# A decoder trunk on one core: in a step of seven products, the fifth goes to SBUF and is added from there

## The chip, the cores and the metric

The kernel runs on one core of one Trainium2 chip. The metric is device time in microseconds (us) of one execution, lower is better. Engines are named as the profile names them: PE is TensorE's matmul side (PEld its weight loads), DVE is VectorE, ACT is ScalarE, POOL is GpSimd, SP is SyncE, which issues most DMAs.

## The reference

The program is a decoder trunk of two layers for one sequence of 512 tokens and a width of 1024, all in float32. Each layer does

```
h = RMSNorm(x)
p = h @ W_in                     # columns shared by four head groups
y = concat[retention(p), conformer_conv(p), gated_deltanet(p), hgrn2(p)]
x = x + y @ W_out
x = x + SwiGLU(RMSNorm(x))       # silu(x @ W_gate) * (x @ W_up), then @ W_down; hidden width 2816
```

and a last RMSNorm follows. The mixers are causal and work in chunks along the sequence. The change lies in the last line, the feed-forward part.

## The kernel before, in words

Activations lie transposed: 128 rows of the width on the partitions, the 512 tokens along the free axis. So x is eight tiles of 128x512, and the hidden width is 22 tiles, j = 0 to 21. A product in float32 is made of two halves of each operand, a high part (rounded to the type fp32r) and the rest: `mm3` issues three matmuls for it, high by high (L461), high weight by low activation (L462), low weight by high activation (L463). Weights come by DMA into `wraw`; ScalarE makes the high half (L257, L383) and GpSimd or VectorE the low half (L258, L384). PSUM has two pools of four banks of 128x512 each: `pm` and `pd`.

**The step of seven products.** In the feed-forward part most tiles are made in pairs by a scheme in the manner of Strassen: the gate and up products of one j, or two output tiles of the down projection, take seven products of half the width (256 tokens) instead of eight. Their names are e, t1, t2, g, h, t3, t4. The weights of these products are the quarters a, b, d of a pair and the differences s1 to s4, which `s_item` computes ahead on VectorE and GpSimd (L366, L370, L374, L378). The activations are sums of token halves, made by `operand` for the gate and up products and by `blocks_even` and `blocks_odd` (with `split`, L1567 to L1569) for the down products. A product is 12 matmuls of 128x256: four blocks by three.

`step` (from L1636) makes one such pair. It takes two banks of `pm`: `ab` and `cd`, each with a lower half LO (256 columns) and an upper half UP. In order:

- e into the lower half of cd; ScalarE copies it to the lower half of gs, in SBUF (L1648)
- t1 into the upper half of ab; ScalarE copies it on (L1650; the change is here)
- `finish()` runs the last part of the step before: its t4 into its cd, and its `second` function
- t2 is accumulated on e in the lower half of cd; ScalarE copies the sum to the upper half of gs (L1653)
- g into the lower, h into the upper half of ab; VectorE adds gs to ab (L1656); `first(ab)` uses the result: Silu into sg on ScalarE for a hidden tile, an addition to x for a down tile
- t3 is accumulated in the lower half of cd; the upper half of cd becomes e+t2+t3 plus t1 (L1659 and L1660; the change is here)
- later, in `end`: t4 is accumulated in the lower half of cd, and `second(cd)` uses the whole bank. For a hidden tile it multiplies with sg (L1677, or in place at L1673) and splits the result for the down products (`hidden_split`, L1583 to L1585 and L1568, L1569); for a down tile it adds to x.

**Where the steps stand.** In each layer j = 0 to 3 are made plainly, j = 4 to 21 by `step` (18 steps), and down tiles by `step` in two parts of four (8 steps), with plain down products (`down_plain`, width 512, into banks of `pd`) for the first and the last tiles. So there are 26 steps in a layer and 52 in the program. Ahead of the feed-forward part of a layer come its mixers, many small operations between dense products: the gated deltanet, called gdn in the code, has chains such as L1082, L1090, L1099, L1112, hgrn2 and the others theirs.

**What sets the order.** Each engine runs its instructions in one fixed order. That order is not the order of the code: the program is built with a scheduler that simulates a timeline (`schedule_with_timeline_sim=True`, L1823) and places instructions by it, within dependencies. An edit therefore also moves instructions that it does not name. The wait of an instruction is for whole tiles or parts of them; a matmul into a half of a bank has to wait for an operation of another engine that writes or reads the bank and stands ahead of it.

Of the kernel before, what the change touches and what calls it, by code (L numbers as in the profile page):

```python
# [7 lines left out]
F32 = mybir.dt.float32  # L8
# [8 lines left out]
P = 128  # L17
# [121 lines left out]
def kernel(  # L139
# [15 lines left out]
    V, S, GP, PE = nc.vector, nc.scalar, nc.gpsimd, nc.tensor  # L155
    MUL, ADD, SUB = ALU.mult, ALU.add, ALU.subtract
# [257 lines left out]
    def w_next(keep=0):  # L414

        i = pos[2]
        pos[2] += 1
        for q in held.values():
            q[:] = [n for n in q if n >= i - keep]
        p = piece_of(items[i])  # L420
        w_split(i + 1)
        assert i in halves
        w_load(p + 3)
        w_split(i + 2)
        while pos[1] < min(i + 1 + AHEAD, len(items)) and len(items[pos[1]]) == 2 and extra:
            n = pos[1]
            w_split(n + 1)
            if pos[1] == n:
                break
            w_load(piece_of(items[n]) + 3)  # L430
        return halves.pop(i)
# [27 lines left out]
    def mm3(ps, hi, lo, kk, ah, al, first, last, shared=False):  # L459
        w = slice(kk * P, (kk + 1) * P)  # L460
        PE.matmul(ps, hi[:, w], ah, start=first, stop=False, skip_group_check=shared)  # L461
        PE.matmul(ps, hi[:, w], al, start=False, stop=False, skip_group_check=shared)  # L462
        PE.matmul(ps, lo[:, w], ah, start=False, stop=last, skip_group_check=shared)  # L463
# [1028 lines left out]
    for l in range(DEPTH):  # L1492
# [47 lines left out]
        with tc.tile_pool(name=f"ffp{l}", bufs=1, reuse_waits="tile") as ffp, \  # L1540
# [3 lines left out]
            HC = T // 2  # L1544
            LO, UP = slice(0, HC), slice(HC, T)
# [84 lines left out]
            def finish():  # L1630

                for f in last:
                    f()
                last.clear()

            def step(of, first, second):  # L1636

                def product(ps, nm, start=False):
                    hi, lo = w_next()
                    for k in range(KD // 2):  # L1640
                        mm3(ps, hi, lo, k, *of(k, nm), start and k == 0, k == KD // 2 - 1, True)

                ab = pm.tile([P, T], F32, name="pm")
                cd = pm.tile([P, T], F32, name="pm")
                gs = fft.tile([P, T], F32, name="gs")
                u3 = fft.tile([P, HC], F32, name="u3")
                product(cd[:, LO], "e", True)
                S.copy(gs[:, LO], cd[:, LO])  # L1648
                product(ab[:, UP], "t1", True)
                S.copy(cd[:, UP], ab[:, UP])  # L1650
                finish()
                product(cd[:, LO], "t2")
                S.copy(gs[:, UP], cd[:, LO])  # L1653
                product(ab[:, LO], "g")
                product(ab[:, UP], "h")
                V.tensor_tensor(ab, ab, gs, op=ADD)  # L1656
                first(ab)
                product(cd[:, LO], "t3")
                S.copy(u3, cd[:, LO])  # L1659
                V.tensor_tensor(cd[:, UP], cd[:, UP], u3, op=ADD)  # L1660

                def end():
                    product(cd[:, LO], "t4")
                    second(cd)
                last.append(end)

            def hidden(j):
                sg = fft.tile([P, T], F32, name="sg")

                def up(cd):  # L1670
                    if j in rest and j != rest[0]:
                        raw[j] = cd
                        V.tensor_tensor(cd, cd, sg, op=MUL)  # L1673
                        hidden_split(j)
                    else:
                        raw[j] = sqp.tile([P, T], F32, name="sq")
                        V.tensor_tensor(raw[j], cd, sg, op=MUL)  # L1677
                        if (j - HEAD) % PART:
                            hidden_split(j)
                step(of_x, lambda ab: S.activation(sg, ab, AF.Silu), up)  # L1680

            def down(part, q):
                def add(m):
                    return lambda ps: V.tensor_tensor(x[m], x[m], ps, op=ADD)
                step(of_hidden, add(2 * q), add(2 * q + 1))
                if q == KD // 2 - 1:

                    last.append(lambda: hidden_split(HEAD + PART * (part + 1)))
# [138 lines left out]
```

## Time and profile before

| | us |
|---|---|
| three runs | 1333.13, 1335.5, 1335.95 |
| median | 1335.5 |
| the profiled execution | 1333.43 |
| its span in the trace | 1331.6 |
| ScalarE instructions in the span | 1454, busy 705.5 |

The mean granted clock of TensorE in the profiled execution was 0.978 of full speed. How rows are read: a row of a timeline has the start in us, the duration in us, engine, line, operation, the tile written and the tiles read, the shape, and in brackets the idle time of the engine ahead of it and what ended that. Tile names are without numbers there, so `pm<-pm` can be two different banks. A row of a source line has the count and the shortest, median and longest duration in ns. A row of waits has the line that waited, the line that it waited for, us in total, times, and the longest in us. Matmuls are pipelined, so their durations overlap: the next one can start before the end of the last.

In the trace the steps of layer 0 run from 383 us to some 655 us, and those of layer 1 from 1030 us to some 1304 us; the mixers of layer 1 lie between some 700 us and 945 us.

### The profile page before, as it was taken

The numbers are of one execution on the slowest core, as the hardware profiler recorded it, in microseconds if no ns is written. First come the engines' busy times: TensorE is split into PE (matmuls) and PEld (weight loads), VectorE is DVE, ScalarE is ACT, GpSimd is POOL, SyncE is SP. The second block draws the span as 40 slices with busy tenths as digits, with TensorE's granted clock in tenths as the row PEclk, the third lists the DMA queues.
The fourth block names the chain that finished last, engine by engine and source line by source line (L and its number), as shares of the span: only waits on it lengthen the run. The fifth ranks groups of instructions, "written<-read, shape, count | busy, mean of one in ns | idle before, by whom it ended". The sixth has DMA issues, their size and how long they took to land.

```text
span 1331.6 us, 23717 instructions
## 1 busy us (share of the span) xinstructions
PE 1287.8 (97%) x8984; PEld 1177.3 (88%) x8984; DVE 897.5 (67%) x1569; ACT 705.5 (53%) x1454; POOL 788.4 (59%) x669
## 2 busy tenths in 40 slices
PE   8999998899999999999999999999999999999996
PEld 6888887888889999999888889889788999999995
DVE  5753778646787867876465448686559777678645
ACT  5553543535456656655545435445444665566554
POOL 6376773753255765676545767747523666566762
PEclk9999998899999999999999999889999999999998
DMA  7223210134043333342542232002423243333322
GB/s 270 79 79 105 75 25 9 41 111 134 25 135 96 111 112 96 97 126 80 164 138 80 81 88 67 25 1 71 154 69 103 80 123 102 110 97 110 122 78 72
DMA packets 60386, 124.52 MB, mean 94 GB/s; under 512 B 17520, under 2 KB 26992, under 8 KB 60272
## 3 DMA queue, kind: packets, MB, share of 16 engines
q1 hardware_dynamic: 58832, 121.83, 30.0%
q8 instruction: 71, 1.16, 0.4%
q10 hardware_dynamic: 1440, 1.18, 0.3%
q14 instruction: 43, 0.35, 0.1%
HBM read 116.17 MB, written 6.82 MB: 92 GB/s over the span
## 4 chain that ended last, share of the span: by engine, by line
PE 82%; DVE 8%; POOL 5%; ACT 3%; issue 2%; DMA 0%; SPq 0%; POOLq 0%; ACTq 0%; DVEq 0%
PE pm L461 12%; PE pm L462 12%; PE pm L463 12%; PE pd L461 10%; PE pd L462 10%; PE pd L463 10%; PE pd L486 2%; PE pm L1189 2%; PE pd L488 2%; PE pd L487 2%; POOL wlo L258 2%; DVE x L1292 1%; PE pm L928 1%; ACT whi L383 1%; PE pm L1062 1%
## 5 line engine op out<-in xcount | busy, mean ns | idle before, releaser
L258 POOL TENSOR_TENSOR wlo<-wraw,whi 128x512 fp32r<-128x512 f32 (+2 forms) x192 | 248.9, 1305 | 227.3 <-ACT whi L257 186.7
L384 POOL TENSOR_TENSOR wlo<-wraw,whi 128x512 fp32r<-128x512 f32 x208 | 272.5, 1329 | 104.4 <-ACT whi L383 99.9
L461 PE MATMUL pm<-bh,whi 128*128 128x256 f32 x1008 | 282.5, 282 | 3.9 <-ACT pm L1650 2.0
L462 PE MATMUL pm<-bl,whi 128*128 128x256 f32 x1008 | 281.2, 280 | 0.0
L463 PE MATMUL pm<-bh,wlo 128*128 128x256 f32 x1008 | 276.5, 280 | 0.0
L257 ACT CAST whi<-wraw 128x512 fp32r<-128x512 f32 (+2 forms) x212 | 125.3, 598 | 188.1 <-PE pd L462 105.1
L461 PEld LDWEIGHTS pm<-bh,whi 128*128 128x128 f32 x1008 | 189.6, 188 | 6.8 <-DVE pm L1660 3.1
L462 PEld LDWEIGHTS pm<-bl,whi 128*128 128x128 f32 x1008 | 190.0, 188 | 0.5
L463 PEld LDWEIGHTS pm<-bh,wlo 128*128 128x128 f32 x1008 | 187.8, 189 | 0.1
L383 ACT CAST whi<-wraw 128x512 fp32r<-128x512 f32 x208 | 126.7, 624 | 50.1 <-PE pm L462 42.7
L461 PE MATMUL pd<-xh,whi 128*128 128x512 f32 x384 | 151.6, 396 | 0.6 <-DVE x L729 0.6
L463 PE MATMUL pd<-xh,wlo 128*128 128x512 f32 x384 | 151.9, 396 | 0.0
L462 PE MATMUL pd<-xl,whi 128*128 128x512 f32 x384 | 151.6, 396 | 0.0
L384 DVE TENSOR_TENSOR wlo<-pd,whi 128x512 fp32r<-128x512 f32 x156 | 107.3, 688 | 52.4 <-ACT whi L383 49.9
L383 ACT CAST whi<-pd 128x512 fp32r<-128x512 f32 x156 | 92.0, 590 | 64.9 <-PE pm L462 22.6
L378 POOL TENSOR_TENSOR wraw<-wraw 128x512 f32<-128x512 f32 x52 | 68.8, 1324 | 78.2 <-DVE pd L366 65.9
L486 PE MATMUL pd<-whi,xh 128*128 128x256 f32 (+1 forms) x320 | 94.2, 295 | 8.0 <-DVE x L1292 3.4
L487 PE MATMUL pd<-wlo,xh 128*128 128x256 f32 (+1 forms) x320 | 93.7, 293 | 0.0
L488 PE MATMUL pd<-whi,xl 128*128 128x256 f32 (+1 forms) x320 | 93.5, 293 | 0.0
L461 PEld LDWEIGHTS pd<-xh,whi 128*128 128x128 f32 x384 | 72.3, 188 | 16.7 <-DVE x L729 0.8
L462 PEld LDWEIGHTS pd<-xl,whi 128*128 128x128 f32 x384 | 72.2, 188 | 16.0
L463 PEld LDWEIGHTS pd<-xh,wlo 128*128 128x128 f32 x384 | 72.2, 188 | 15.9
(359 smaller groups left out, 3181.0 us busy)
## 6 DMA issues: line engine op xcount, KB each, us to landing
wraw<-in_wf_dram SPq DMA_DIRECT2D x88, 512.0 KB, 3.6
wraw<-in_wc_dram SPq DMA_DIRECT2D x34, 512.0 KB, 3.6
wraw<-in_wd_dram SPq DMA_DIRECT2D x32, 512.0 KB, 4.0
wraw<-in_wt_dram SPq DMA_DIRECT2D x16, 512.0 KB, 3.6
wraw<-in_wo_dram SPq DMA_DIRECT2D x32, 256.0 KB, 2.6
x<-in_xt_dram SPq DMA_DIRECT2D x16, 256.0 KB, 3.7
wraw<-in_wd_dram SPq DMA_DIRECT2D x16, 256.0 KB, 2.7
wraw<-in_wd_dram SPq DMA_DIRECT2D x20, 128.0 KB, 2.0
```

What stands on the lines that cost most here:

```text
L257: S.copy(hi[:, :n], r)
L258: eng.tensor_tensor(lo[:, :n], r, hi[:, :n].bitcast(F32), op=SUB)
L378: GP.tensor_tensor(src, c, a, op=SUB)
L383: S.copy(hi, src)
L384: eng.tensor_tensor(lo, src, hi.bitcast(F32), op=SUB)
L461: PE.matmul(ps, hi[:, w], ah, start=first, stop=False, skip_group_check=shared)
L462: PE.matmul(ps, hi[:, w], al, start=False, stop=False, skip_group_check=shared)
L463: PE.matmul(ps, lo[:, w], ah, start=False, stop=last, skip_group_check=shared)
L486: PE.matmul(o, xh[k][:, tk], hi[:, w], start=(k == 0 and first), stop=False)
L487: PE.matmul(o, xh[k][:, tk], lo[:, w], start=False, stop=False)
L488: PE.matmul(o, xl[k][:, tk], hi[:, w], start=False, stop=(k == KD - 1 and last))
L1189: PE.matmul(ps[:, (bb * 2 + ct) * P:(bb * 2 + ct + 1) * P], k[:, ct * T + b * P:ct * T + (b + 1) * P], qx[:, (ct * NB + b) * P:(ct * NB + ...
```

## The change: t1 to SBUF, one addition instead of copy and addition

Before, ScalarE copied t1 from its bank ab into the upper half of the bank cd, and after t3 it copied the lower half of cd to an SBUF tile u3, which VectorE added to the upper half. Now ScalarE copies t1 to an SBUF tile p5 (same size, same pool, two buffers), and after t3 VectorE writes the sum of the lower half of cd and p5 to the upper half. The second copy is gone. What is computed stays the same.

```diff
                 gs = fft.tile([P, T], F32, name="gs")
-                u3 = fft.tile([P, HC], F32, name="u3")
+                p5 = fft.tile([P, HC], F32, name="u3")
                 product(cd[:, LO], "e", True)
                 S.copy(gs[:, LO], cd[:, LO])
                 product(ab[:, UP], "t1", True)
-                S.copy(cd[:, UP], ab[:, UP])
+                S.copy(p5, ab[:, UP])
                 finish()
...
                 product(cd[:, LO], "t3")
-                S.copy(u3, cd[:, LO])
-                V.tensor_tensor(cd[:, UP], cd[:, UP], u3, op=ADD)
+                V.tensor_tensor(cd[:, UP], cd[:, LO], p5, op=ADD)
```

The changed file is one line shorter there, so L1660 of before is L1659 of after. ScalarE has 52 copies fewer; the other engines have the same instructions in another order. TensorE's order is the same up to the first steps of layer 0; from there on the steps, and the mixers of layer 1, are placed anew. Four places show it.

First TensorE, from the end of t1 of j=7 on. Before, pm_4154 is ab and pm_4155 is cd of j=7, pm_4007 is cd of j=6, and a row with waits names the engine that the matmul waits for:

```order
L463 MATMUL pm_4154<-bh3_3174,wlo_4081 128x256
L461 MATMUL pm_4155<-bh0_3168,whi_4115 128x256 [waits Activation_49]
...
L463 MATMUL pm_4155<-bh3_3174,wlo_4116 128x256
L461 MATMUL pm_4154<-bh0_3168,whi_4135 128x256
L462 MATMUL pm_4154<-bl0_3169,whi_4135 128x256
L461 MATMUL pm_4007<-bh0_3168,whi_4099 128x256 [waits DVE_49]
```

After, the same tiles are pm_4151 (ab), pm_4152 (cd of j=7) and pm_4005 (cd of j=6):

```order
L463 MATMUL pm_4151<-bh3_3174,wlo_4079 128x256
L461 MATMUL pm_4005<-bh0_3168,whi_4097 128x256 [waits DVE_49,Activation_49]
...
L463 MATMUL pm_4005<-bh3_3174,wlo_4098 128x256
L461 MATMUL pm_4152<-bh0_3168,whi_4113 128x256 [waits Activation_49]
...
L463 MATMUL pm_4152<-bh3_3174,wlo_4114 128x256
L461 MATMUL pm_4151<-bh0_3168,whi_4133 128x256 [waits Activation_49]
```

Before, t2 of j=7 follows t1 directly, and t4 of j=6 comes after it, between the matmuls of g; after, t4 of j=6 stands between t1 and t2.

Second VectorE, in the step of j=8. Before, pm_4297 is ab and pm_4298 is cd; the rows of L384, L370 and L374 work on weights of later products:

```order
L384 TENSOR_TENSOR wlo_4372<-pd_4373,whi_4371 128x512 [waits Activation_49]
L370 TENSOR_TENSOR pd_4408<-wraw_4199,pd_4373 128x512 [waits DMAHW7_49]
L1656 TENSOR_TENSOR pm_4297<-pm_4297,gs_4299 128x512 [waits PE_49]
L384 TENSOR_TENSOR wlo_4407<-pd_4408,whi_4406 128x512 [waits Activation_49]
L374 TENSOR_TENSOR pd_4451<-wraw_4199,pd_4408 128x512 [waits DVE_49]
L1660 TENSOR_TENSOR pm_4298<-pm_4298,u3_4300 128x256 [waits Activation_49]
```

After, they are pm_4293 and pm_4294:

```order
L384 TENSOR_TENSOR wlo_4368<-pd_4369,whi_4367 128x512 [waits Activation_49]
L370 TENSOR_TENSOR pd_4404<-wraw_4196,pd_4369 128x512 [waits DMAHW7_49]
L1656 TENSOR_TENSOR pm_4293<-pm_4293,gs_4295 128x512 [waits PE_49]
L1659 TENSOR_TENSOR pm_4294<-pm_4294,u3_4296 128x256 [waits PE_49]
L384 TENSOR_TENSOR wlo_4403<-pd_4404,whi_4402 128x512 [waits Activation_49]
L374 TENSOR_TENSOR pd_4446<-wraw_4196,pd_4404 128x512 [waits DVE_49]
```

The addition into the upper half now follows L1656 directly and waits for TensorE; L384 and L374 come behind it.

Third TensorE at the end of the steps of layer 0. Before, pm_7258 is cd of j=21; the first row is the end of its t3, the row with whi_7356 the start of its t4, and the last row the first plain down product that needs the result (ph6):

```order
L463 MATMUL pm_7258<-bh3_3174,wlo_7281 128x256
L462 MATMUL pd_7420<-ph1_3177,whi_7404 128x512
...
L462 MATMUL pd_7472<-ph5_3181,whi_7449 128x512
L461 MATMUL pm_7258<-bh0_3168,whi_7356 128x256 [waits DVE_49]
...
L463 MATMUL pm_7258<-bh3_3174,wlo_7357 128x256
L463 MATMUL pd_7472<-ph4_3180,wlo_7450 128x512
L461 MATMUL pd_7374<-ph6_3182,whi_7383 128x512 [waits Activation_49]
```

After, the bank is pm_7233:

```order
L463 MATMUL pm_7233<-bh3_3174,wlo_7256 128x256
L462 MATMUL pd_7348<-ph3_3179,whi_7327 128x512
...
L463 MATMUL pd_7394<-ph4_3180,wlo_7379 128x512
L461 MATMUL pm_7233<-bh0_3168,whi_7331 128x256 [waits DVE_49]
...
L463 MATMUL pm_7233<-bh3_3174,wlo_7332 128x256
L463 MATMUL pd_7420<-ph0_3176,wlo_7398 128x512 [waits Pool_49]
...
L463 MATMUL pd_7446<-ph4_3180,wlo_7424 128x512
L461 MATMUL pd_7348<-ph6_3182,whi_7357 128x512 [waits Activation_49]
```

Between t3 and t4 there were 25 plain down matmuls and are now 16; between t4 and the first matmul that reads ph6 there was one and are now 16.

Fourth, TensorE in the mixers of layer 1, at a chain of the gated deltanet. Before, with dense products into banks of pd between the links:

```order
L1189 MATMUL pm_8880<-ar4_7_8648,ar4_3_8117 128x128 [waits PE_49]
...
L463 MATMUL pd_9362<-xh6_90,wlo_9261 128x512
...
L461 MATMUL pd_9492<-xh5_89,whi_9358 128x512
L1090 MATMUL pm_8892<-ar2_7_8410,ar2_10_8415 128x64 [waits DVE_49,PE_49]
...
L462 MATMUL pd_9492<-xl5_97,whi_9358 128x512
...
L463 MATMUL pd_9492<-xh7_91,wlo_9359 128x512
L1099 MATMUL pm_8907<-ar2_7_8410,ar4_3_8140 128x128 [waits Activation_49]
```

After, with further matmuls of the same lines left out:

```order
L1082 MATMUL pm_8847<-gS0_175,ar4_1_7682 128x128 [waits DVE_49]
...
L1189 MATMUL pm_8854<-ar4_7_8622,ar4_3_8091 128x128 [waits PE_49]
...
L1090 MATMUL pm_8866<-ar2_7_8384,ar2_10_8389 128x64 [waits DVE_49,Activation_49]
...
L1099 MATMUL pm_8881<-ar2_7_8384,ar4_3_8114 128x128 [waits Activation_49]
...
L1112 MATMUL pm_8888<-ar2_7_8384,ar2_1_7595 128x64 [waits DVE_49]
```

Before, 20 dense matmuls (width 512) stood between L1189 and L1090, and 8 between L1090 and L1099; they now come ahead of the chain.

## The prediction

> **What bounds the kernel now.** I read the page first (busy times, chain), then the windows of the feed-forward stages, then what TensorE waited for, and last the timelines around those waits.
>
> ```profile
> span 1331.6 us, 23717 instructions
> PE 1287.8 (97%) x8984; PEld 1177.3 (88%) x8984; DVE 897.5 (67%) x1569; ACT 705.5 (53%) x1454; POOL 788.4 (59%) x669
> PE 82%; DVE 8%; POOL 5%; ACT 3%; issue 2%; DMA 0%; SPq 0%; POOLq 0%; ACTq 0%; DVEq 0%
> ```
>
> TensorE is busy for 97% of the span and makes up 82% of the chain that ended last. The next two rows are stretches of feed-forward steps, one in each layer (columns: busy time of PE, PEld, DVE, ACT, POOL with counts; granted clock; DMA share; GB/s).
>
> ```profile
> 404.00:640.00 236.00, 234.20 (x1970) 232.62 (x1969) 170.40 (x281) 143.77 (x309) 152.85 (x118) 1.00 0.34 101
> 1060.00:1300.00 240.00, 238.08 (x1986) 235.51 (x1985) 169.42 (x279) 145.35 (x311) 157.03 (x121) 1.00 0.35 104
> ```
>
> In the steps TensorE idles 1.8 and 1.9 us in about 240, at full clock; a matmul follows the last after 234.20 / 1970 = 0.119 us. The change removes no matmul, so all that it can gain there is idle time of TensorE. That time is named in the waits of PE (us in total, times, longest):
>
> ```profile
> PE pd L461 <- ACT ph L1568: 2.3, 2, 1.2
> PE pm L461 <- ACT pm L1650: 2.0, 4, 0.5
> PE pm L461 <- DVE pm L1660: 1.9, 6, 0.4
> ```
>
> Twelve waits, 6.2 us together. All three kinds hang on lines that the edit touches: the copy of the fifth product, the addition into the upper half, and the chain behind the last t4.
>
> **Part by part: the copies.** These rows give the lines' cost (ns min/median/max), the last one for how long VectorE sat idle ahead of the addition, and how often, until the copy L1659 was done.
>
> ```profile
> L1650 ACT COPY pm<-pm x52: 357/375/396, 386.2 to 1287.3; 128x256 f32<-128x256 f32 x52
> L1659 ACT COPY u<-pm x52: 365/372/380, 395.5 to 1296.7; 128x256 f32<-128x256 f32 x52
> L1660 DVE TENSOR_TENSOR pm<-pm,u x52: 418/432/433, 396.0 to 1297.1; 128x256 f32<-128x256 f32 x52
>   ACT u L1659: 22.4, 27
> ```
>
> The t1 copy now writes SBUF as L1659 did, so I price it at 0.372 instead of 0.375 us: nothing. L1659's 52 copies go: 52 x 0.372 = 19.3 us of ScalarE. ScalarE is busy 53%, so by itself this gives nothing; it counts only where a matmul waited behind it. The addition keeps its shape, one PSUM and one SBUF operand: 0.432 us as before. Its wait is new: for TensorE's last t3 matmul, not for ScalarE. Behind it in VectorE's queue stand weight splits (L384, L374) for products still to come; at those 27 places the addition starts earlier by the copy's 0.4 us, so they come no later. At the others VectorE has a backlog and the addition waits for nothing: nothing again.
>
> **Place 1: t2 behind the t1 copy** (j=7; four such waits in the kernel).
>
> ```profile
> 415.89 0.28 PE L463 MATMUL pm<-bh,wlo 128*128 128x256 f32 x1
> 416.26 0.36 ACT L1650 COPY pm<-pm 128x256 f32<-128x256 f32 x1 [0.20 <-PE pm L463]
> 416.67 0.39 PE L461 MATMUL pm<-bh,whi 128*128 128x256 f32 x1 [0.50 <-ACT pm L1650]
> 416.90 0.28 PE L462 MATMUL pm<-bl,whi 128*128 128x256 f32 x1
> ```
>
> The copy wrote the upper half of the bank into whose lower half t2 goes, so t2 waited. The wait costs more than its 0.50: from 415.89 to 416.90 are two intervals, 1.01 - 2 x 0.119 = 0.77, so 0.27 us of restart comes with it. I add 0.27 to each of the twelve. In the changed order the copy no longer touches that bank, and t2 of j=7 depends on it no more; what still waits for it is the next writer of the bank that it reads (g or h). The nearest of these stands 14 matmuls behind t1, 14 x 0.119 = 1.67 us, against 416.67 - 415.89 = 0.78 that the copy needed here from the last t1 matmul to the release. Gain 2.0 + 4 x 0.27 = 3.1 us.
>
> **Place 2: t4 close behind t3** (j=4 of each layer).
>
> ```profile
> 395.55 0.38 ACT L1659 COPY u<-pm 128x256 f32<-128x256 f32 x1
> 395.93 0.28 PE L462 MATMUL pm<-bl,whi 128*128 128x256 f32 x1
> 395.96 0.43 DVE L1660 TENSOR_TENSOR pm<-pm,u 128x256 f32<-128x256 f32 x1 [0.62 <-ACT u L1659]
> 396.45 0.39 PE L461 MATMUL pm<-bh,whi 128*128 128x256 f32 x1 [0.23 <-DVE pm L1660]
> ```
>
> The chain copy, addition, t4 loses its first link, 395.96 - 395.55 = 0.41 us, more than the 0.23 waited. In the changed order 24 instead of 12 matmuls also stand between t3 and this t4, 1.4 us more. Both waits go.
>
> **Place 3: the addition late in VectorE's queue** (j=8; four such waits, behind odd j whose splits fill VectorE).
>
> ```profile
> 428.28 0.69 DVE L1677 TENSOR_TENSOR sq<-pm,sg 128x512 f32<-128x512 f32 x1
> 435.26 0.38 ACT L1659 COPY u<-pm 128x256 f32<-128x256 f32 x1
> 435.40 0.69 DVE L384 TENSOR_TENSOR wlo<-pd,whi 128x512 fp32r<-128x512 f32 x1
> 436.01 0.69 DVE L374 TENSOR_TENSOR pd<-wraw,pd 128x512 f32<-128x512 f32 x1
> 436.46 0.28 PE L463 MATMUL pm<-bh,wlo 128*128 128x256 f32 x1
> 436.60 0.42 DVE L1660 TENSOR_TENSOR pm<-pm,u 128x256 f32<-128x256 f32 x1
> 437.08 0.38 PE L461 MATMUL pm<-bh,whi 128*128 128x256 f32 x1 [0.34 <-DVE pm L1660]
> ```
>
> Here the copy was done by 435.64; the addition started only at 436.60, after L384 and L374. So dropping the copy would gain nothing: what gains is that the new order puts the addition ahead of those two, 436.60 - 435.40 = 1.20 us earlier, against 0.34 waited. With place 2 the six waits on L1660 give 1.9 + 6 x 0.27 = 3.5 us.
>
> **Place 4: the end of the steps** (last t4 of each layer, before the plain down products).
>
> ```profile
> 653.80 0.28 PE L463 MATMUL pm<-bh,wlo 128*128 128x256 f32 x1
> 654.11 0.70 DVE L1673 TENSOR_TENSOR pm<-pm,sg 128x512 f32<-128x512 f32 x1 [5.96 <-PE pm L463]
> 655.48 1.19 PE L461 MATMUL pd<-ph,whi 128*128 128x512 f32 x4 [1.17 <-ACT ph L1568]
> ```
>
> From the last t4 matmul to the first that needs its result pass 655.48 - 653.80 = 1.68 us, with one matmul to fill them. Now sixteen matmuls of double width stand there, 16 x 2 x 0.119 = 3.8 us, since t4 comes earlier (16 of them instead of 25 behind t3; the addition needs 0.5 of those). Gain 2.3 + 2 x 0.27 = 2.9 us. Together 3.1 + 3.5 + 2.9 = 9.5 us.
>
> **What it may cost.** First, t4 of j=6 now comes 60 matmul intervals after the last of t4 of j=5, 60 x 0.119 = 7.1 us, instead of 78. VectorE needs for its list there:
>
> ```profile
> 408.71 0.69 DVE L1677 TENSOR_TENSOR sq<-pm,sg 128x512 f32<-128x512 f32 x1 [3.14 <-PE pm L463]
> 412.86 0.68 DVE L384 TENSOR_TENSOR wlo<-pd,whi 128x512 fp32r<-128x512 f32 x1
> ```
>
> A start delay as at 653.80 to 654.11, 0.31; then 412.86 - 408.71 = 4.15; then three operations of 0.60 apart (435.40 to 436.01), 0.43 for the addition and 437.08 - 436.60 - 0.42 = 0.06 to release: 6.75 us. That leaves 0.4 of slack; I charge 0.2 a layer, 0.4, with ends 0 and 2.4 (the 1.2 of place 3 in each layer). Second, layer 1's mixers get another order, since their weights are split elsewhere on ScalarE. One gdn chain lies in the way of this:
>
> ```profile
> 184.77 0.71 PE L1099 MATMUL pm<-ar,ar 128*128 128x128 f32 x4 [0.46 <-ACT ar L1092]
> 828.49 1.06 PE L1189 MATMUL pm<-ar,ar 128*128 128x128 f32 x8
> 834.04 1.00 PE L1090 MATMUL pm<-ar,ar 128*128 128x64 f32 x8
> 836.80 0.38 PE L1099 MATMUL pm<-ar,ar 128*128 128x128 f32 x2
> 845.15 0.50 PE L461 MATMUL pd<-xh,whi 128*128 128x512 f32 x1 [0.60 <-DVE x L729]
> ```
>
> In layer 1, 28 dense matmuls stood between L1189, L1090 and L1099 and no wait showed; now the chain's links follow each other directly, as they do in layer 0, where L1099 waited 0.46. The dense work is done earlier, not lost, and may fill other waits (the 0.60 at 845.15). Ends: -1.0 (that wait and its restart gone, 0.9), and +6.2, all of 828.49 to 836.80 less the two runs of matmuls in it (8.31 - 1.06 - 1.00). I take +1.0, two waits of layer 0's size, as the row of the same chain is the nearest. All other distances from t1 to g and from t3 to t4 are as long or longer than before, or at least 1.4 us.
>
> **The sum.** -9.5 + 0.4 + 1.0 = -8.1 on the profiled execution's 1333.4 us (span 1331.6): 1325.3. The median of the three runs lies 2.1 above it, so the forecast is 1335.5 - 8.1, about **1327.5 us**, likeliest 1324 to 1330.
>
> One term stays out of the sum, the granted clock. Three stretches of layer 1's mixers (columns as above):
>
> ```profile
> 836.80:844.50 7.70, 7.70 (x69) 7.56 (x67) 4.26 (x10) 3.19 (x6) 7.70 (x8) 1.00 0.22 64
> 857.40:874.40 17.00, 16.27 (x97) 15.06 (x96) 11.97 (x21) 6.50 (x13) 5.85 (x5) 0.50 0.02 8
> 925.80:929.20 3.40, 3.40 (x20) 3.17 (x20) 2.39 (x6) 1.00 (x2) 0.00 (x0) 0.52 0.02 5
> ```
>
> Two of them ran at 0.50, though TensorE was busy for 16.27 of 17 us and for all of 3.4. Which stretches fall there may shift when the order of layer 1 does; the first row, the small matmuls that follow the chain above without dense work between, kept 1.00. 3.4 us at half clock hold 1.7 us of work at full, so one such stretch more or less moves the time by 1.7 us.
>
> By the Trainium skill, "TensorE: Matmul & The Clock Gate", section "Part 1: The HAM clock gate (the "warmup" mystery)", half rate follows an idle window of about 3.4 us. The trace does not agree at 857 to 874, where 0.73 us were idle in 17 at 0.50. By that rule a new order without idle windows slows nothing, and the range would lose what it has for the clock.
>
> **The rivals.** (1) *The addition stays late.* If VectorE, not the copy or its place in the queue, sets t4 (place 3 everywhere, and j=6's slack used up), the 3.5 us on L1660 stay and 0.8 more come: -9.5 + 3.5 + 0.4 + 1.0 + 0.8 = -3.8, **1331.7**. For it: the copy at 435.26 was not what was late. Against: the order has the addition 1.2 us earlier. (2) *The clock shifts* by two stretches, 3.4 us: **1324 or 1331**. For it: 20.4 us of layer 1's mixers ran at 0.50, and the links of the gdn chain now stand in one row with the small matmuls after them. Against: these kept 1.00. (3) *The waits only move.* The copy frees t2, but g and h, which write the bank it reads, wait in its place, and the shortened chains meet something else: **1335**. Against: 1.67 us of cover at the nearest. That 52 copies are gone and nothing gains belongs here.
>
> The Trainium skill, "PSUM — Partial Sum Buffer", section "PSUM bank collisions raise a hardware error", has software keep two engines off one bank and quadrant, disjoint columns too; by that rule t2's wait at 416.67 is the copy's doing, which the trace bears out, and the wait moves to g or h, up to the 1335 of (3) where nothing covers it; covered, the time stays 1327.5.
>
> (4) *Slower: layer 1's mixer chain uncovered.* The dense matmuls that hid the gdn chain run too early, all 6.2 us open up, TensorE idles, and the stretch from 828 to 845 goes to 0.50 as 857 to 874 did. With 6.2 us idle and 17 us at half clock (8.5 us of work late) the change ends at -9.5 + 0.4 + 6.2 + 8.5 = +5.6, **1341.1**. It decides once more than 9.1 + 2.7 = 11.8 us are lost there. For it: layer 0's same chain waits; against: only 0.46.
>
> **How the numbers follow.** 0.2% is 2.7 us, about what a measurement of this kernel can tell. Forecast 0.67; late addition 0.12; clock 0.12 (half at 1324, half at 1331); moved waits 0.05; slower 0.04. Range 1322 to 1333: the forecast's lower end less one stretch of the clock (1324 - 1.7), and above the late addition with its own spread; outside lie the moved waits, the slower case and the edges, under 0.2. Faster by over 0.2% (below 1332.8): 0.67 + 0.09 of the late addition + 0.10 of the clock = 0.86; the same 0.05 + 0.03 + 0.01 = 0.09; slower 0.04 + 0.01 of the clock = 0.05.
>
> **What would show it.** Right: no waits of PE on the t1 copy (now 2.0), on the L1660 addition (1.9) or on L1568 (2.3), ScalarE some 19 us less busy, idle time of TensorE in the two stretches under 0.5 us, and layer 1's mixer at most 2 us longer. Wrong: waits on the addition as many as before; g or h waiting for the copy; or layer 1's mixer longer by more than 6 us or at a lower clock.

## The result and the profile after

| | before | after |
|---|---|---|
| four runs each, median | 1335.07 us (1333.13 to 1335.95) | 1320.69 us (1317.79 to 1323.68) |
| ratio of the runs | | 0.9894, 95% interval 0.9867 to 0.9922 |
| the profiled execution, span | 1333.43, 1331.6 | 1323.68, 1321.5 |

The change makes the kernel faster by 14.4 us by the medians, interval 10.4 to 17.8. The forecast was 8.0 us faster (1327.5), its range 1322 to 1333: the direction was right, the size too small, and the median lies 1.3 us below the range. Between the two profiles the gain is 10.1 us of span. So there are two questions: why the profiles show 10.1 and not 8.1, and why the medians show 14.4 when the two profiled executions are 9.75 apart.

The page of after: span and busy times.

```profile
span 1321.5 us, 23710 instructions
PE 1286.7 (97%) x8984; PEld 1179.7 (89%) x8984; DVE 900.5 (68%) x1569; ACT 689.8 (52%) x1402; POOL 789.3 (60%) x669
```

ScalarE is 705.5 - 689.8 = 15.7 us less busy, with 52 instructions fewer. That is less than the 52 x 0.372 = 19.3 us of the copies, because rows of ScalarE overlap (in before a cast of 0.60 us starts at 426.87 and the next at 427.34) and busy time counts an overlap once. The next view is the windows of the two stretches of steps, as for before.

```profile
404.00:640.00 236.00, 236.00 (x2001) 235.84 (x2000) 171.77 (x283) 139.18 (x290) 155.31 (x120) 1.00 0.34 103
1060.00:1300.00 240.00, 240.00 (x1986) 237.65 (x1985) 168.21 (x278) 139.57 (x289) 156.10 (x121) 1.00 0.35 104
```

TensorE's idle time there went from 1.8 and 1.9 us to none. The steps get shorter by more than that, as the parts below show: a matmul of this size lasts 0.28 us by its row and the next follows after 0.12, so the first 0.16 us of a pause does not appear as idle time. In the list of its waits the three lines of before (copy, addition, L1568) are gone. The source view of the addition, L1659 now, has this row of its own and one for the idle time ahead of it:

```profile
L1659 DVE TENSOR_TENSOR pm<-pm,u x52: 415/425/433, 394.8 to 1287.1; 128x256 f32<-128x256 f32 x52
  PE pm L463: 7.1, 12
```

VectorE stood idle for it 12 times, 7.1 us, until TensorE's t3; before it was 27 times, 22.4 us, until ScalarE's copy. At the end of layer 0's steps the timeline is now:

```profile
646.31 0.28 PE L463 MATMUL pm<-bh,wlo 128*128 128x256 f32 x1
646.43 0.40 PE L463 MATMUL pd<-ph,wlo 128*128 128x512 f32 x1
646.69 0.70 DVE L1672 TENSOR_TENSOR pm<-pm,sg 128x512 f32<-128x512 f32 x1 [4.75 <-PE pm L463]
650.12 1.09 PE L461 MATMUL pd<-ph,whi 128*128 128x512 f32 x4
```

The last t4 matmul, the down products that now follow it, the multiplication on VectorE 0.38 us behind it (0.31 before), and the first group that takes its result (650.12) without a bracket: no idle time ahead of it.

**Where the time went, by parts of the span.** These rows are the first matmul of the first step and the last plain down matmul of each layer, before:

```profile
381.70 0.28 PE L461 MATMUL pm<-bh,whi 128*128 128x256 f32 x1
669.27 0.40 PE L463 MATMUL pd<-ph,wlo 128*128 128x512 f32 x1
1031.39 0.28 PE L461 MATMUL pm<-bh,whi 128*128 128x256 f32 x1
1318.83 0.28 PE L463 MATMUL pd<-ph,wlo 128*128 128x256 f32 x1
```

and after:

```profile
381.64 0.28 PE L461 MATMUL pm<-bh,whi 128*128 128x256 f32 x1
663.82 0.39 PE L463 MATMUL pd<-ph,wlo 128*128 128x512 f32 x1
1027.20 0.28 PE L461 MATMUL pm<-bh,whi 128*128 128x256 f32 x1
1309.59 0.28 PE L463 MATMUL pd<-ph,wlo 128*128 128x256 f32 x1
```

| part | before | after | difference |
|---|---|---|---|
| start to the first step | 381.70 | 381.64 | -0.06 |
| layer 0, first step to last down matmul | 287.57 | 282.18 | -5.39 |
| from there to layer 1's first step (its mixers) | 362.12 | 363.38 | +1.26 |
| layer 1, first step to last down matmul | 287.44 | 282.39 | -5.05 |
| the end | 12.77 | 11.91 | -0.86 |

The gain sits where the forecast had it, in the steps of both layers: 10.44 us, against 9.1 forecast there (9.5 less 0.4). The mixers' part is 1.26 longer, against 1.0 forecast; whether the new order is the reason is taken up below.

### The profile page after: what moved, and what is told of

It is laid out like the page before. It is cut to its first block, busy times and chain, and to the rows that moved or that the text cites. A ratio compares the mean times of both kernels' runs of the same rounds, so it can differ in the third digit from the quotient of the medians.

```text
span 1321.5 us, 23710 instructions
## 1 busy us (share of the span) xinstructions
PE 1286.7 (97%) x8984; PEld 1179.7 (89%) x8984; DVE 900.5 (68%) x1569; ACT 689.8 (52%) x1402; POOL 789.3 (60%) x669
## 4 chain that ended last, share of the span: by engine, by line
PE 88%; DVE 5%; POOL 3%; ACT 2%; issue 1%; DMA 0%; SPq 0%; POOLq 0%; DVEq 0%; ACTq 0%
PE pm L462 13%; PE pm L461 13%; PE pm L463 13%; PE pd L461 10%; PE pd L462 10%; PE pd L463 10%; PE pm L1189 2%; PE pd L488 2%; PE pd L486 2%; PE pd L487 2%; PE pm L928 1%; DVE x L1292 1%; POOL wlo L258 1%; PE pm L1051 1%; DVE ar L623 1%
## 5 line engine op out<-in xcount | busy, mean ns | idle before, releaser
L384 POOL TENSOR_TENSOR wlo<-wraw,whi 128x512 fp32r<-128x512 f32 x208 | 272.6, 1328 | 105.2 <-ACT whi L383 101.1
L384 DVE TENSOR_TENSOR wlo<-pd,whi 128x512 fp32r<-128x512 f32 x156 | 107.0, 686 | 62.5 <-ACT whi L383 59.6
```

Of the source, the lines that this page charges most:

```text
L384: eng.tensor_tensor(lo, src, hi.bitcast(F32), op=SUB)
```

## The experiments

Times of one kernel spread: over all runs the changed kernel went from 1317.8 to 1327.2 us, and the mean granted clock of a run from 0.975 to 0.983 with it. So beside each median stands a difference **at the same clock**: a fit of all 125 runs of this study that list their clock (10 kernels; the changed kernel's two sets and layer0's two taken together), with a level for each kernel and one common slope. The slope is -0.84 us (standard error 0.05) for 0.001 more of clock, the scatter left is 1.4 us. The changed kernel, ten runs, lies 10.6 +- 0.5 us below the kernel before at the same clock (raw means: 11.1). The +- are standard errors. A second measure needs no such correction: the length of the two step parts of the table above in each kernel's profile, where the granted clock was 1.00 in every one. Together they are 575.01 us before and 564.57 after, -10.4.

### The changed kernel again, and one layer at a time

again: no edit.

> The changed kernel once more, for its spread. Theory S (steps): between the two profiles each layer's feed-forward part is 5.4 and 5.05 us shorter to its last down product, the end 0.9, and layer 1's mixers 1.3 longer, -10.1 in all; what the medians show beyond that (-14.4 over four runs) is the state of the clock from run to run. Then the feed-forward parts of the new profile are again 282.2 and 282.4 us, and what differs from the first profile lies in the mixers, in stretches at half clock; the median is 1319 to 1325. Rival M (mixers): the new order of layer 1's mixers is itself some 4 us quicker in the usual run and the first profile was an unlucky one. Then the part from layer 0's last down product to layer 1's first step is 358 to 360 us (363.4 in the first profile, 362.1 before), and the median stays at or under 1321.

Measured: median 1323.71 us (1318.63 to 1327.20, six runs), ratio 0.9920 (0.9902 to 0.9938), 1325.0 us of span in its profile. In that profile the two step parts are 282.18 and 282.69 us, as expected of S within 0.3; what differs more is the part ahead of the first step, 383.0 us (381.6 in the first profile), and the mixers' part, 365.22 us (363.38). M's 358 to 360 us did not show, and the median is above its 1321. The first four runs of the changed kernel were a quick draw.

layer0 and layer1: the change in one layer; in the other the two lines of before. For layer0:

```diff
-                S.copy(p5, ab[:, UP])
+                S.copy(p5 if l == 0 else cd[:, UP], ab[:, UP])
...
-                V.tensor_tensor(cd[:, UP], cd[:, LO], p5, op=ADD)
+                if l == 0:
+                    V.tensor_tensor(cd[:, UP], cd[:, LO], p5, op=ADD)
+                else:
+                    S.copy(p5, cd[:, LO])
+                    V.tensor_tensor(cd[:, UP], cd[:, UP], p5, op=ADD)
```

> The change in layer 0 only; layer 1's mixers get the same order as with the whole change, layer 1's steps stay as before. Theory S: -5.4 in layer 0's steps and +1.3 in layer 1's mixers: 4.1 us less than before, 1331. Rival M: the mixers' new order gives some 3 to 4 us more: 1326.5 to 1328, 7 to 8.5 less than before.

> The change in layer 1 only; layer 1's mixers keep their order of before. Theory S: -5.05 in layer 1's steps and -0.9 at the end: 5.9 us less than before, 1329. Rival M says the same here, 1329, since the mixers are those of before; the two differ in the other kernel of this pair. A gain of 9 us or more would be against both.

Measured: layer1 1329.13 us, ratio 0.9961 (0.9949 to 0.9973), as both theories had it; at the same clock -5.0 +- 0.6. layer0 1325.96 us, ratio 0.9939 (0.9927 to 0.9951): by the median M's number, not S's 1331. But all five runs had a clock of 0.981 to 0.983, where the kernel before had 0.9786 in the mean. At the same clock, with the second set below, layer0 lies 4.7 +- 0.4 us below before. S had -4.1, M -7 to -8.5. The two profiles of this kernel show what is missing to 5.4: layer 0's steps take 282.2 us as in the changed kernel, and the mixers' part 361.4 and 362.6 beside 362.1 before, but layer 1's steps take 288.2 us in both, 0.8 more than before, with TensorE in the order of before. The 0.8 lies spread over the whole part and in no one wait; its cause is open. The two layers add up: 4.7 + 5.0 = 9.7 beside 10.6.

layer0_b: the same kernel once more.

> The kernel with the change in layer 0 only, once more: its first five runs had a mean clock of 0.982, where the changed kernel has 0.979 with the same order up to layer 1's steps. Theory K (chance): the clock of a job's runs is not the kernel's own; then the mean clock is nearer 0.979 now and the time 1327 to 1330. Rival M2 (own clock): the kernel has the higher clock again, 0.981 or more, and 1324.5 to 1327.

Measured: 1326.99 us, nine runs, mean clock 0.9804. That lies between the two expectations (0.979 and 0.981), so whether this kernel has a clock of its own is not settled.

### Which half of the change does it?

t1_only: t1 to SBUF, but the copy after t3 kept (u3 a tile of its own, with one buffer).

```diff
                 product(cd[:, LO], "t3")
-                V.tensor_tensor(cd[:, UP], cd[:, LO], p5, op=ADD)
+                S.copy(u3, cd[:, LO])
+                V.tensor_tensor(cd[:, UP], u3, p5, op=ADD)
```

> t1 goes to SBUF, but the copy of the lower half after t3 stays, and VectorE adds two SBUF tiles: half of the change. Theory S: the gain comes from t2 and the bank being free of the t1 copy and from the order that follows; the 52 copies on ScalarE are off the path. Then it is within 1 us of the changed kernel, with no wait on the t1 copy and at most 0.5 us on the addition. Rival C (copies): the 52 copies, 19.3 us of ScalarE, or the copy's 0.41 us in the chain to t4, carry what the forecast missed. Then it is 2 us or more slower than the changed kernel, and waits of 1 us or more on the addition remain.

Measured: 1327.84 us, ratio 0.9953 (0.9940 to 0.9965), -4.4 +- 0.6 at the same clock: 6 us slower than the changed kernel. That is what C said and not S. But the source view of its addition shows a second change that came with the edit (the row, then who waited for it):

```profile
L1661 DVE TENSOR_TENSOR pm<-u,p x52: 423/1270/1653, 393.3 to 1292.1; 128x256 f32<-128x256 f32 x52
...
  PEld pm L461: 5.3, 14
  PE pm L461: 1.9, 7
```

With both operands in SBUF the addition took 1.27 us in the median, not 0.43. Two of them, with what GpSimd did at the time:

```profile
410.54 2.56 POOL L384 TENSOR_TENSOR wlo<-wraw,whi 128x512 fp32r<-128x512 f32 x2
412.07 1.31 DVE L1661 TENSOR_TENSOR pm<-u,p 128x256 f32<-128x256 f32 x1
413.44 0.39 PE L461 MATMUL pm<-bh,whi 128*128 128x256 f32 x1 [0.45 <-DVE pm L1661]
...
430.33 1.31 POOL L384 TENSOR_TENSOR wlo<-wraw,whi 128x512 fp32r<-128x512 f32 x1
431.73 0.42 DVE L1661 TENSOR_TENSOR pm<-u,p 128x256 f32<-128x256 f32 x1
```

The first ran beside GpSimd's two subtractions from SBUF and took 1.31 us; the second began when GpSimd had just ended, and took 0.42. The Trainium skill, "SBUF — State Buffer", section "Who interferes with whom", says that a VectorE instruction with two SBUF inputs contends with a GpSimd instruction that reads SBUF; these rows agree. So this kernel did not test the copy alone.

chain_copy does: the copy stays in the chain, but the addition keeps one PSUM operand.

```diff
                 product(cd[:, LO], "t3")
-                V.tensor_tensor(cd[:, UP], cd[:, LO], p5, op=ADD)
+                S.copy(cd[:, UP], cd[:, LO])
+                V.tensor_tensor(cd[:, UP], cd[:, UP], p5, op=ADD)
```

> t1 goes to SBUF as in the change, but after t3 ScalarE still copies the lower half of cd, now to its upper half, and VectorE adds the SBUF tile there: the addition keeps one PSUM operand and the copy stays in the chain to t4. TensorE's order is that of the kernel in which VectorE added two SBUF tiles (there the addition took 1.27 us instead of 0.43). Theory T (chain): the copy counts where it stands ahead of the addition, as the order puts the addition behind other work when it has to wait for ScalarE. Then waits on the addition remain, 4 to 7 a layer of 0.2 to 0.4 us, and the time is 2 to 4 us above the changed kernel's at the same clock (1324.5 to 1326.5 beside 1322.4). Rival D (slow addition): the two SBUF operands alone made that kernel slow; then no waits of over 0.2 us remain and the time is within 1 us of the changed kernel. Rival L (load): what counts is 19 us of ScalarE; then it is as slow as the kernel with 52 idle copies.

Measured: 1319.65 us, ratio 0.9894 (0.9869 to 0.9920), -11.3 +- 0.6 at the same clock: as quick as the changed kernel. The copy and the addition in its profile:

```profile
L1659 ACT COPY pm<-pm x52: 357/367/386, 395.5 to 1285.4; 128x256 f32<-128x256 f32 x52
L1660 DVE TENSOR_TENSOR pm<-pm,u x52: 418/432/433, 395.9 to 1285.8; 128x256 f32<-128x256 f32 x52
  ACT pm L1659: 22.6, 34
```

All 52 copies are there, VectorE waits for them 34 times and 22.6 us, and no wait of TensorE on the addition is left in its list. As in the changed kernel, the order has the addition of j=8 directly behind L1656, ahead of the weight splits:

```profile
433.03 0.69 DVE L1656 TENSOR_TENSOR pm<-pm,gs 128x512 f32<-128x512 f32 x1
433.63 0.42 DVE L1660 TENSOR_TENSOR pm<-pm,u 128x256 f32<-128x256 f32 x1
433.96 0.68 DVE L384 TENSOR_TENSOR wlo<-pd,whi 128x512 fp32r<-128x512 f32 x1
```

TensorE's order is that of t1_only but for the place of the last t4 of each layer, and the steps take 10.3 us less than before, where t1_only's take 4.1 less. Rival D is right, theory T falls: the 6 us of t1_only were the slow addition, and once t1 goes to SBUF, dropping the copy gives nothing more.

idle_copies: 52 copies of that size more on ScalarE, of no use to anyone.

```diff
                 V.tensor_tensor(cd[:, UP], cd[:, LO], p5, op=ADD)
+                S.copy(gs[:, LO], p5)
```

> The changed kernel with 52 more copies of the same size on ScalarE, from the SBUF tile p5 to gs behind the addition, which nothing uses; TensorE's order is that of the changed kernel. Theory T: ScalarE is off the path; the time is within 1 us of the changed kernel at the same clock, 1322.4, and no wait appears in the steps. Rival L (load): 2 us or more slower, with waits of TensorE on ScalarE's weight casts or copies.

Measured: 1320.79 us, ratio 0.9911 (0.9891 to 0.9930), -11.3 +- 0.6 at the same clock. ScalarE is back at its old load and it costs nothing:

```profile
PE 1280.5 (97%) x8984; PEld 1174.9 (89%) x8984; DVE 900.3 (68%) x1569; ACT 705.3 (53%) x1454; POOL 789.1 (60%) x669
```

### Is it the dependency of t2, or the order?

bank_wait: the changed kernel, but t2 has to wait for ScalarE again.

```diff
                 S.copy(p5, ab[:, UP])
+                S.copy(cd[:, HC:HC + 1], ab[:, HC:HC + 1])
```

> The changed kernel, and behind the t1 copy a second copy of one column into the upper half of cd (overwritten later), so that t2 has to wait for ScalarE as before. The order answers this: t2 never follows t1 directly, at least 12 matmuls (1.4 us) stand between, so that by the distances no wait on the copy shows. Theory O (order): the dependency alone costs nothing where the order covers it; the four waits of before were a choice of the order. Then no wait on the copy, and the time is within 2 us of the changed kernel at the same clock (1322 to 1324.5). Rival P: the dependency itself costs; the waits on the copy come back and the time is 3 us or more above the changed kernel.

Measured: 1324.18 us, ratio 0.9928 (0.9906 to 0.9950), -8.4 +- 0.6 at the same clock. No wait on the copy or the addition is in its list, as O expected; with the dependency there the order puts other products between t1 and t2. It lacks 2.2 +- 0.7 us to the changed kernel. In its profile the steps are 0.4 us longer in each layer (282.58 and 282.84), and one kind of wait is left, at their end:

```profile
PE pd L461 <- ACT ph L1568: 1.1, 2, 0.5
```

Half of the 2.3 us of before is still there, 1.1 + 2 x 0.27 = 1.6 us with the restarts, though the steps are longer by 0.85 only. The rest of the 2.2 is not placed. Its mixers have the order of before. This kernel stands for the other half of the change: dropping the copy with t1 still in cd's upper half was not tried, since the addition would then read both operands from PSUM.

both_kept: this and chain_copy's edit together, so that both dependencies of before are back.

```diff
                 S.copy(p5, ab[:, UP])
+                S.copy(cd[:, HC:HC + 1], ab[:, HC:HC + 1])
...
-                V.tensor_tensor(cd[:, UP], cd[:, LO], p5, op=ADD)
+                S.copy(cd[:, UP], cd[:, LO])
+                V.tensor_tensor(cd[:, UP], cd[:, UP], p5, op=ADD)
```

> The changed kernel with both of its dependencies put back: a one-column copy into cd's upper half behind the t1 copy, so that t2 waits for ScalarE, and the copy of cd's lower half (to the upper half) ahead of the addition. Each alone left no wait in the steps. TensorE's order is now nearly that of before: t2 follows t1 at once at the same four places. Theory O (order): the gain hangs on the order, which is bad only when both dependencies are there. Then the waits on the copy come back at four places (2.0 us before, somewhat more with the second copy), those on the addition at 4 to 6, the two at the end of the steps with 2.3, and the time is that of before, 1333 to 1336, at the same clock. Rival S2 (separate costs): each dependency costs what it cost alone, 0 and 2.5 us; then 1324 to 1326.

Measured: 1335.14 us, twelve runs, ratio 1.0003 (0.9982 to 1.0025), +1.2 +- 0.4 at the same clock. The waits are back:

```profile
PE pm L461 <- ACT pm L1651: 3.1, 8, 0.5
PE pd L461 <- ACT ph L1568: 2.4, 2, 1.2
PE pm L461 <- DVE pm L1661: 0.5, 2, 0.2
```

TensorE waits for the copy at t2, and the addition of j=8 stands behind L384 and L374 again, as in before:

```profile
410.95 0.38 PE L461 MATMUL pm<-bh,whi 128*128 128x256 f32 x1 [0.53 <-ACT pm L1651]
...
437.57 0.69 DVE L1657 TENSOR_TENSOR pm<-pm,gs 128x512 f32<-128x512 f32 x1
438.32 0.69 DVE L384 TENSOR_TENSOR wlo<-pd,whi 128x512 fp32r<-128x512 f32 x1
438.92 0.69 DVE L374 TENSOR_TENSOR pd<-wraw,pd 128x512 f32<-128x512 f32 x1
439.61 0.43 DVE L1661 TENSOR_TENSOR pm<-pm,u 128x256 f32<-128x256 f32 x1
```

That is O in the time and in the order, and S2 (1324 to 1326) falls. The shares differ from O's: eight waits on the copy instead of four, and two on the addition instead of four to six. Four kernels make a square; each field has the difference from before at the same clock, and that of the steps in the profile:

| | addition straight from t3 | copy of t3's sum ahead of it |
|---|---|---|
| t2 free of ScalarE | -10.6, steps -10.4 (the change) | -11.3, steps -10.3 |
| t2 waits for ScalarE | -8.4, steps -9.6 | +1.2, steps -0.1 |

Either half alone gives most of the gain; only with both dependencies does the scheduler arrive at the order that waits. Why it does so then was not tried.

fin_early: the order changed by hand in the kernel before. In this kernel t1 and the t4 of the step before take each other's weights, so it computes something else with the same amount of work.

```diff
-                product(ab[:, UP], "t1", True)
-                S.copy(cd[:, UP], ab[:, UP])
                 finish()
+                product(ab[:, UP], "t1", True)
+                S.copy(cd[:, UP], ab[:, UP])
```

> The kernel before with one line moved: the last part of the step before (t4) comes ahead of t1 in the code. The order that follows has two places in the program where t2 follows t1 at once instead of four. Theory O: each place whose t2 gets distance loses its wait, 0.77 us: waits on the copy fall from 2.0 to 1.0 us; waits on the addition stay near 1.9, and the time falls by 1 to 3 us against before (1331 to 1333). Rival P: no gain, 1334, as the data flow is that of before.

Measured: 1334.10 us, ratio 1.0007 (0.9990 to 1.0024), +2.3 +- 0.5 at the same clock.

```profile
PE pm L461 <- ACT pm L1651: 1.0, 2, 0.5
PE pm L461 <- DVE pm L1660: 1.0, 4, 0.4
PE pm L461 <- ACT whi L383: 0.6, 2, 0.4
PE pm L461 <- ACT sg L1680: 0.3, 1, 0.3
```

Each place that got distance lost its wait on the copy, 2.0 to 1.0 us, as O said; those on the addition fell too, where O had them stay near 1.9. Yet the time did not fall: it is P's 1334, and in the profile the steps are 1.1 and 1.8 us longer than before. The list does not explain that: with the new waits on weight casts and on sg it comes to 5.2 us (2.3 of them at the end of the steps, as before) against 6.2. What came in shows at the weight loads, which wait also where the list of PE has nothing (before has none of these three rows):

```profile
PEld pm L461 <- ACT whi L383: 1.6, 5, 0.6
PEld pm L461 <- ACT sg L1680: 0.8, 2, 0.5
PEld pm L463 <- POOL wlo L384: 0.5, 2, 0.3
```

An order that removes a wait by hand can make others.

## Why the prediction was right or wrong, step by step

- **TensorE bounds the steps and the gain is its lost time: right.** Idle 1.8 and 1.9 us went to none, the steps got 10.4 us shorter, and ScalarE's load does not matter (idle_copies: 705.3 us busy again, no cost).
- **Place 1, t2 free of the copy, 3.1 us: right in the outcome, the reason too narrow.** The wait went, and g and h did not take it over. But it also goes when t2 still has to wait (bank_wait), because the order then covers it.
- **Place 2 and 3, the addition, 3.5 us: right that its place in VectorE's queue counts and not the copy** (chain_copy: copy kept, addition early, waits gone). But the copy is not without effect: with t2 waiting for ScalarE, dropping it is worth 9.5 us of the steps (both_kept against bank_wait), because the order then changes. **The term was too small.** I counted the six waits in the list of PE. The source view of the addition before shows who waited for it:

```profile
  PEld pm L461: 4.2, 10
  PE pm L461: 1.9, 6
```

  Ten weight loads waited, not six. One of the four others, in the timeline of before:

```profile
476.84 0.43 DVE L1660 TENSOR_TENSOR pm<-pm,u 128x256 f32<-128x256 f32 x1 [0.68 <-ACT u L1659]
476.96 0.28 PE L462 MATMUL pm<-ph,whi 128*128 128x256 f32 x1
477.33 0.39 PE L461 MATMUL pm<-ph,whi 128*128 128x256 f32 x1
```

  The row at 477.33 has no bracket, so the list of waits leaves it out, but 0.37 us lie between two matmuls that stand 0.12 apart otherwise: 0.25 lost. The four together cost 0.25 + 0.23 + 0.24 + 0.24 = 0.96 us, and are gone after. The matmul behind each is late by another 0.10, so with these they come to 1.4, which is 0.4 more than the steps' total leaves room for: the split is good to about that. So the term was 3.5 us and measured 4.5 to 4.9.
- **Place 4, the end of the steps, 2.9 us (2 x 1.17 + 2 x 0.27): right** (646.31 to 650.12 above).
- **The third step, +0.4: not spent.** t4 of j=6 did not wait; the margin of 0.4 us that the rows gave held.
- **Layer 1's mixers, +1.0: right for the chain, and luck for the total.** The chain waited as its like in layer 0 does:

```profile
833.20 1.07 PE L1090 MATMUL pm<-ar,ar 128*128 128x64 f32 x8 [0.43 <-DVE ar L1086]
834.74 0.71 PE L1099 MATMUL pm<-ar,ar 128*128 128x128 f32 x4 [0.46 <-ACT ar L1092]
```

  But the wait of 0.60 us on L729 is gone in exchange, and the +1.26 between the two profiles does not show a cost of the order: eight profiles with the new order of this part (all kernels here but before, layer1, bank_wait and both_kept) have 360.7 to 365.2 us in it, three with that of before 361.8 to 365.6. Before's profile had a granted clock of 0.972 there and after's 0.967; at 0.981 it took 361.8 us in the old order (bank_wait) and 360.7 to 361.4 in the new.
- **The end, not in the sum: -0.86.** The last matmuls of the program, before and after:

```profile
1321.69 1.22 PE L242 MATMUL pm<-cs,rst 128*128 128x128 f32 x4 [0.47 <-POOL rst L213]
```

```profile
1312.46 0.71 PE L242 MATMUL pm<-cs,rst 128*128 128x128 f32 x4 [0.47 <-POOL rst L213]
```

  The same four matmuls took 1.22 us and then 0.71: before, they fell into a stretch at half clock (granted 0.50 from 1321.6 to 1323.0; after, 1.00 from 1312.4 to 1313.2). This accounts for 0.5 of the 0.86. That it is chance and not the change is likely, not shown: profiles of the other kernels have 11.7 to 12.9 us for this part.
- **The sum, -8.1: the profiles gave -10.1.** The difference is the four short waits (-1.0), the 0.4 not spent, the end (-0.9) and the mixers (+0.3); only the first two, in the steps, are the change's own. At the same clock the change is worth 10.6 +- 0.5 us.
- **The step that failed most: "The median of the three runs lies 2.1 above it, so the forecast is 1335.5 - 8.1".** It carries the profile's place among the runs of before over to after. After's median was put 2.1 us above its profile, and it lies 3.0 below: the profiled execution was the slowest of the four. That is 2.1 + 3.0 = 5.1 of the 6.8 us between 1327.5 and 1320.69, and it is scatter: six more runs of the same kernel had the median 1323.71, inside the range. The other 1.7 is the gain that was sized too small, 9.75 us between the profiled executions against 8.1.
- **The range** had one stretch of half clock below the forecast (1.7 us) and nothing for a gain that was sized too small. The runs show the clock's part to be larger: at 0.84 us for 0.001, the changed kernel's 0.975 to 0.983 are 6.7 us. That the clock would differ at all was seen; in after, too, a stretch of some 17 us of the mixers ran at 0.50:

```profile
853.80:870.90 17.10, 16.64 (x97) 14.95 (x96) 11.75 (x20) 6.49 (x13) 5.91 (x5) 0.50 0.04 15
```

- **The rivals.** The late addition (1) and the moved waits (3) did not come: no wait in the steps. The uncovered chain (4) came to 0.9 us of waits, not 6.2. The clock (2) moves single runs by its 3.4 us and more, in both kernels; as a part of the change it was not shown.

## What to carry to other kernels

Where a scheduler sets the order, an edit to a dependency is worth what the new order makes of it: read the two orders side by side at the places that wait, and don't price the removed instruction. Size the gain from the source view of the line that is waited for, weight loads included, and not from the list of waits alone, which leaves out short ones. Before a median of a few runs is set beside a sum made on one profile, look at how far the runs of one kernel spread with their clock. Where the stretch that was changed ran at full clock, compare its length alone: in layer 0 the new steps took 282.17 to 282.20 us in the five profiles with this order, while ten runs of the changed kernel spread over 9.4.

## What the runs showed of the hardware that was not expected

- An addition of 128x256 on VectorE took 0.43 us with one operand in PSUM, and 0.42 to 1.65 us, median 1.27, with both in SBUF beside a busy GpSimd.
- A matmul that waits loses more than the list shows: 0.26 to 0.27 us more with each of the twelve waits of before. Of this 0.16 is the pause that the row of the matmul ahead, 0.28 us long where the next comes after 0.12, still covers, and 0.10 is the lateness of the matmul behind it (0.23 us instead of 0.12 from 416.67 to 416.90). The four pauses of 0.23 to 0.25 us above are not named in the list at all.
- Runs of one kernel differ by up to 12 us with the mean granted clock (both_kept: 1327.04 at 0.986 to 1339.39 at 0.975), 0.84 us for 0.001, with the same instructions in the same order.
